# Both MLPs' matrix products by seven products of quarters in place of eight

## The chip, the cores and the metric

The kernel runs on one core of one Trainium2 chip. The metric is the device time of one launch in microseconds (us). Before the change it is 2720.57 us, the median of three runs (2720.34 to 2721.82).

The engines are named as in the profile: PE does matrix products (PEld loads their weights), DVE, ACT and POOL work on vectors, SP issues most of the DMA transfers. A queue with a q behind the name (SPq) is that engine's instruction queue.

## The reference, cut to what matters

Two transformer blocks run one after the other on 1024 tokens of width 1024. Each ends in an MLP of width 4096, with a residual; the attention and mixer parts ahead of the MLPs, the norms and the final norm are not touched by the change.

```
# block 1
h = rmsnorm(x, g_mlp)
hid = square(relu(h @ w_mlp_in))          # [1024,1024] @ [1024,4096]
x = x + hid @ w_mlp_out                   # [1024,4096] @ [4096,1024]
# block 2: mod = silu(c) @ w_ada + b_ada, cut in six (sh1, sc1, gt1, sh2, sc2, gt2)
x = x + gt1 * mixer(rmsnorm(x) * (1 + sc1) + sh1)
h = rmsnorm(x, g_ffn) * (1 + sc2) + sh2
x = x + gt2 * (square(relu(h @ w_ff1)) @ w_ff2)
return rmsnorm(x)
```

Everything is float32. A float32 product is made of three faster ones: each operand is cut into a rounded part `hi` and the rest `lo`, and hi·hi, hi·lo and lo·hi are summed.

## The kernel before, in words

All activations lie transposed, features on the 128 partitions and tokens along the rows; `xT[hf]` holds the residual of token half hf (512 tokens), as 8 tiles of 128x512, and `HT[hf]` the normed input h as `hi` and `lo`. `gemm_T` (L421 to L423) issues, for each 128 rows of the inner dimension, three PE instructions of 128x128 weights by 128x512 activations. `wunit` fetches a block of weights (`wload`, L132: one DMA on SP), ACT casts it into `wh` (L133), and DVE, in some places POOL, subtracts that from it for `wl` (L134).

One function, `mlp`, does both MLPs. It goes over the width 4096 in eight chunks of 512. In a chunk the first product makes four tiles of hidden values (`g1`): for each half the 24 PE instructions, then relu from PSUM on ACT (L1159), square on DVE (L1161), the `hi` cast on ACT (L1162) and `lo` on DVE (L1163). They stay in SBUF. Then the second product goes over the 8 output tiles, each from 4 weight tiles, for both halves; DVE adds the result from PSUM to the residual (`upd`, L1066, or L1068 with the gate of block 2). In the last chunk the sums of squares for the next norm are collected (`Stat.add`, with a POOL addition, L1011, and DVE instructions such as L1009), and in block 2 the output is turned back.

Ahead of each MLP stands the output projection (`out_proj`). Its second half leaves work that `mlp` starts in its first chunk through `begin`: the norm's factor is spread over the partitions (L1037), and `make_h` (L1076 and L1080, in block 2 L1083) makes h of token half 1 on DVE and ACT. Until then PE works on token half 0. In block 1 the MLP also carries `ada`, the product of silu(c) with `w_ada`: 48 loads of 512 KB on SP and as many DVE instructions (L1136), in small steps (`tick`).

Each engine has one queue in program order. The order in which instructions of different parts stand in it was fixed by the scheduler that builds the program, from the order of the code; on the chip an instruction at the head of a queue that waits holds up all behind it.

Of the kernel before, what the change touches and what calls it, by code (L numbers as in the profile page):

```python
# [60 lines left out]
def block_kernel(ctx, tc, x, mem, positions, g_mix, w_in, b_gate, sinks, g_mem, w_mem_kv, w_proj_swa, w_proj_dsa,  # L61
# [1055 lines left out]
    def ada(modp):  # L1117
# [10 lines left out]
        for g in range(6):  # L1128
            acc = modp([P, D], tag="ada", bufs=1)
            for k in range(DC):  # L1130
                w = modp([P, D], tag="adaw", bufs=2)
# [6 lines left out]
            m8 = mod[:, g * 8:(g + 1) * 8]  # L1138
            for j0 in (0, 4):
                pt = tp_bank()  # L1140
                for j in range(4):
                    T.transpose(pt[:, j * P:(j + 1) * P], acc[:, (j0 + j) * P:(j0 + j + 1) * P], ident)
                V.tensor_reduce(m8[:, j0:j0 + 4], pt.rearrange("p (j q) -> p j q", j=4), axis=AX.X, op=OP.add)
            V.tensor_tensor(m8, m8, bada[:, g * 8:(g + 1) * 8], op=OP.add)

    def mlp(pool, w1, w2, upd, post, begin, tick=lambda: None, gains=None, each=lambda i, e: None,
# [4 lines left out]
        NC_ = DFF // 512  # L1151

        def g1(units, f, hfs, hid, mid=None):
            accs = [(hf, mm_bank()) for hf in hfs]
            gemm_T(accs, units, h_rhs, mid=mid)
            for hf, a in accs:
                sl = halves(hf)
                r = pool([P, 512], tag="ml_r", bufs=2)
                A.activation(r, a, AF.Relu)  # L1159
                q = pool([P, 512], tag="ml_q", bufs=2)  # L1160
                V.tensor_tensor(q, r, r, op=OP.mult)  # L1161
                A.copy(hid[f][0][:, sl], q)  # L1162
                V.tensor_tensor(hid[f][1][:, sl], q, raw(hid[f][0][:, sl]), op=OP.subtract)  # L1163

        for c in range(NC_):
            hid = [(pool([P, S], F32R, tag="hid_hi", bufs=4), pool([P, S], F32R, tag="hid_lo", bufs=4))
                   for _ in range(4)]
            if c == 0:
                us = [[wunit(w1, 0, DC, f * P, P)] for f in range(3)]
                for hf in range(2):  # L1170
                    for f in range(3):
                        g1(us[f], f, [hf], hid, begin[1] if (hf, f) == (0, 1) else None)
                        if (hf, f) == (0, 0):
                            begin[0]()
                g1([wunit(w1, 0, DC, 3 * P, P)], 3, [0, 1], hid)
# [5 lines left out]
            def rhs(k, hf):  # L1181
                return hid[k][0][:, halves(hf)], hid[k][1][:, halves(hf)]
            if c < NC_ - 1:
                for e in range(DC):
                    u = [wunit(w2, c * 4, 4, e * P, P)]
                    accs = [(hf, mm_bank()) for hf in range(2)]
                    gemm_T(accs, u, rhs)
                    for hf, a in accs:
                        upd(e, hf, a)
                    if e % 2:  # L1190
                        tick()
            else:
                prev = None
                for i, (hf, t0, n) in enumerate(parts):
                    st = Stat(pools["stm"], gains, n)
                    sl = slice(t0, t0 + n)
                    for e2 in range(DC // 2):
                        hi, lo = wunit(w2, c * 4, 4, e2 * 256, 256, G)
                        for e in range(2):
                            a = mm_bank()[:, :n]  # L1200
                            gemm_T([(hf, a)], [(hi[:, :, e * P:(e + 1) * P], lo[:, :, e * P:(e + 1) * P])],
                                   lambda k, hf: tuple(z[:, sl] for z in rhs(k, hf)))
                            if e2 or e:
# [580 lines left out]
```

## Time and profile before

| what | value |
|---|---|
| median of three runs | 2720.57 us |
| the profiled execution, its own time | 2720.76 us |
| its span, first to last instruction | 2719.0 us |
| PE busy | 2650.9 us, 97% |
| DVE, ACT, POOL busy | 1439.7, 919.0, 339.1 us (53%, 34%, 12%) |
| MLP of block 1, first relu (L1159) to last residual addition (L1066) | starts 884.0 and 1596.0 us |
| MLP of block 2, first relu to last residual addition (L1068) | starts 2001.3 and 2709.9 us |
| DMA, mean over the span | 76 GB/s |

The profile counts an engine as busy while an instruction runs on it, waiting for a lock or a port included. The end of a matrix product is modelled, so one shows about 0.39 us although the next starts after 0.23; the time of a series is read from the starts. The granted clock of PE is a share of full speed, 1.00 being 2.4 GHz and 0.50 being 1.2 GHz.

### The profile page before, as it was taken

The page shows a single profiled execution, that of the slowest core. Times are in us where ns is not written, and L with a number is a line of the kernel's source. Part 1 is how long each engine was busy: PE and PEld are TensorE (multiplying, and loading weights), DVE is VectorE, ACT ScalarE, POOL GpSimd, SP SyncE. Part 2 cuts the span into 40 slices and gives each one's busy share as a digit, 9 for nine tenths or more (in the row PEclk, how much of TensorE's full clock was granted, in tenths as well). Part 3 has the DMA queues.
Part 4 walks back from the last instruction along what each step waited for, and adds up shares of the span by engine and source line. Part 5 has one row for each costly group of instructions (what it writes and reads, how often), then busy time and mean ns, then how long its engine had stood idle before and what let it go on. Part 6 is the DMA issues. An engine that isn't in the chain of part 4 may idle for free.

```text
span 2719.0 us, 34329 instructions
## 1 busy us (share of the span) xinstructions
PE 2650.9 (97%) x13328; PEld 2227.8 (82%) x13328; DVE 1439.7 (53%) x2836; ACT 919.0 (34%) x1826; POOL 339.1 (12%) x337
## 2 busy tenths in 40 slices
PE   7999999899999999999999989999999999999997
PEld 6899987788878888888888867888788888888886
DVE  7685878834455634553453476556553333333335
ACT  6575764335334221222212232332432122211223
POOL 3011123321001000000000331111310000000006
PEclk9999999999999999999999999999999999999999
DMA  3121022311154313331331124221421211121123
GB/s 114 53 61 40 26 80 88 93 57 41 63 165 124 109 45 114 117 102 49 109 101 55 55 59 148 63 78 39 139 70 54 59 36 47 51 58 47 39 62 124
DMA packets 263735, 206.41 MB, mean 76 GB/s; under 512 B 9468, under 2 KB 239636, under 8 KB 263572
## 3 DMA queue, kind: packets, MB, share of 16 engines
q1 hardware_dynamic: 255108, 180.25, 22.0%
q10 hardware_dynamic: 8464, 23.96, 2.6%
q8 instruction: 105, 1.72, 0.3%
q14 instruction: 58, 0.48, 0.1%
HBM read 185.24 MB, written 18.94 MB: 75 GB/s over the span
## 4 chain that ended last, share of the span: by engine, by line
PE 70%; DVE 4%; DMA 2%; ACT 1%; issue 1%; POOL 1%; POOLq 0%; SPq 0%; ACTq 0%; DVEq 0%
PE mm L422 19%; PE mm L423 19%; PE mm L421 19%; PE mm L1304 2%; PE mm L1306 2%; PE mm L1305 2%; PE tp L914 1%; DVE st_acc L1009 1%; PE mm L902 1%; DMA adaw<-in_w_ada_dram 1%; DVE h_lo L1083 0%; ACT wh L133 0%; DVE t L1076 0%; PE fl L273 0%; PE fl L271 0%
## 5 line engine op out<-in xcount | busy, mean ns | idle before, releaser
L423 PE MATMUL mm<-h_hi,wl 128*128 128x512 f32 x1248 | 486.0, 389 | 1.1 <-POOL wl L134 1.1
L133 ACT CAST wh<-wr 128x1024 fp32r<-128x1024 f32 (+3 forms) x303 | 254.8, 842 | 687.3 <-PE mm L422 579.5
L421 PE MATMUL mm<-h_hi,wh 128*128 128x512 f32 x1248 | 486.3, 390 | 0.6 <-ACT ft L280 0.6
L422 PE MATMUL mm<-h_lo,wh 128*128 128x512 f32 x1248 | 485.6, 389 | 0.0
L422 PE MATMUL mm<-hid_lo,wh 128*128 128x512 f32 (+1 forms) x1056 | 405.4, 384 | 3.7 <-DVE hid_lo L1163 3.7
L421 PE MATMUL mm<-hid_hi,wh 128*128 128x512 f32 (+1 forms) x1056 | 407.2, 386 | 0.0
L423 PE MATMUL mm<-hid_hi,wl 128*128 128x512 f32 (+1 forms) x1056 | 404.9, 383 | 0.0
L1161 DVE TENSOR_TENSOR ml_q<-ml_r 128x512 f32<-128x512 f32 x128 | 88.1, 688 | 419.5 <-ACT ml_r L1159 419.5
L134 POOL TENSOR_TENSOR wl<-wr,wh 128x1024 fp32r<-128x1024 f32 (+5 forms) x60 | 124.0, 2070 | 1465.7 <-ACT wh L133 1464.0
L423 PEld LDWEIGHTS mm<-h_hi,wl 128*128 128x128 f32 x1248 | 234.3, 188 | 51.3 <-POOL wl L134 2.0
L421 PEld LDWEIGHTS mm<-h_hi,wh 128*128 128x128 f32 x1248 | 234.3, 188 | 49.6 <-ACT ft L280 0.8
L422 PEld LDWEIGHTS mm<-h_lo,wh 128*128 128x128 f32 x1248 | 234.3, 188 | 48.4
L134 DVE TENSOR_TENSOR wl<-wr,wh 128x1024 fp32r<-128x1024 f32 (+2 forms) x243 | 235.5, 969 | 49.7 <-ACT wh L133 46.0
L422 PEld LDWEIGHTS mm<-hid_lo,wh 128*128 128x128 f32 x1056 | 198.8, 188 | 43.4 <-DVE hid_lo L1163 5.2
L423 PEld LDWEIGHTS mm<-hid_hi,wl 128*128 128x128 f32 x1056 | 198.8, 188 | 38.8
L421 PEld LDWEIGHTS mm<-hid_hi,wh 128*128 128x128 f32 x1056 | 198.8, 188 | 38.6
L1159 ACT ACTIVATE ml_r<-mm 128x512 f32<-128x512 f32 x128 | 76.8, 600 | 448.4 <-PE mm L423 448.4
L1068 DVE SCALAR_TENSOR_TENSOR x<-mm,mod,x 128x512 f32<-128x512 f32 (+1 forms) x152 | 105.7, 722 | 224.0 <-PE mm L423 224.0
L1304 PE MATMUL mm<-h_hi,wh 128*128 128x512 f32 x320 | 132.1, 413 | 0.5 <-DVE kn L1337 0.5
L1306 PE MATMUL mm<-h_hi,wl 128*128 128x512 f32 x320 | 126.7, 396 | 3.3 <-DVE wl L134 3.3
L1305 PE MATMUL mm<-h_lo,wh 128*128 128x512 f32 x320 | 126.0, 394 | 0.0
L1066 DVE TENSOR_TENSOR h_hi<-mm,h_hi 128x512 f32<-128x512 f32 x72 | 49.6, 689 | 124.5 <-PE mm L423 124.5
(474 smaller groups left out, 4573.8 us busy)
## 6 DMA issues: line engine op xcount, KB each, us to landing
adaw<-in_w_ada_dram SPq DMA_DIRECT2D x48, 512.0 KB
wr<-in_w_ff_dram SPq DMA_DIRECT2D x44, 512.0 KB
wr<-in_w_in_dram SPq DMA_DIRECT2D x42, 512.0 KB
wr<-in_w_out_dram SPq DMA_DIRECT2D x32, 512.0 KB
wr<-in_w_mlp_in_dram SPq DMA_DIRECT2D x32, 512.0 KB
wr<-in_w_mlp_out_dram SPq DMA_DIRECT2D x56, 256.0 KB
wr<-in_w_ff_dram SPq DMA_DIRECT2D x56, 256.0 KB
wr<-in_w_in_dram SPq DMA_DIRECT2D x20, 256.0 KB
```

What stands on the lines that cost most here:

```text
L133: A.copy(hi, r)
L134: (eng or V).tensor_tensor(lo, r, raw(hi), op=OP.subtract)
L421: mm(a, hi, r_hi, start=(i == 0), stop=False)
L422: mm(a, hi, r_lo, start=False, stop=False)
L423: mm(a, lo, r_hi, start=False, stop=(i == n - 1))
L1066: V.tensor_tensor(d, a, d, op=OP.add)
L1068: V.scalar_tensor_tensor(d, a, scale[:, e:e + 1], d, op0=OP.mult, op1=OP.add)
L1159: A.activation(r, a, AF.Relu)
L1161: V.tensor_tensor(q, r, r, op=OP.mult)
L1304: mm(a, hi[:, k, :], r_hi, start=(k == 0), stop=False)
L1305: mm(a, hi[:, k, :], r_lo, start=False, stop=False)
L1306: mm(a, lo[:, k, :], r_hi, start=False, stop=(k == DC - 1))
```

## The change

Both products of both MLPs are cut into quarters: inner dimension and output dimension in two, as 2x2 blocks, with the tokens as the other matrix's columns, again in two. One level of Strassen's scheme (in the form with reused sums) makes the four result blocks from seven products of blocks instead of eight. The price is sums and differences of the operands and of the results.

**First product.** The eight inputs are prepared once. `make_h` still makes h of token half 0 (B11, B21). For half 1 a new function `make_t` makes the four other operands as `hi` and `lo` tiles: T1, t2, t3, t4, of which t2 to t4 (`TQ`) go to a new pool. The loop then has 16 turns `m`, each for 128 rows of both output quarters. A turn loads three weight blocks of 512 KB: `e2` (as `wr`), `e1` (as `we`, one buffer) and, through `first_two` for a later turn, the block of `e1` a second time (as `wr`). POOL makes four weight sums of 128x512 (L1272 to L1275). Seven products follow, of 12 PE instructions each (84 in a turn; before, 96 for the same rows). Their sums are five DVE additions from PSUM (L1259, L1284, L1289, L1294, L1301), one DVE addition in SBUF, and a POOL addition (L1285); relu and square now stand on ACT. Four further POOL subtractions (L1305 three times, L1307) make the operands of the second product from the hidden values. The seven resulting tiles of 256 KB go to DRAM (`save`, L1247, on SP).

**Second product.** It goes over the width in four chunks. In each the seven operands are read back (1 MB each), cast on ACT and split, one half on DVE, the other on POOL (L1333); the four weight quarters (1 MB each) get eight 128x1024 sums on POOL; the seven products have 48 PE instructions each (336 in a chunk; before 384 for the same width). DVE adds results to the residual and to `U`, and POOL adds `U` to the residual (`upd_u`, L1352).

**Moved along.** The residual is saved to DRAM in `out_proj` and read back between the two products, since its tiles serve as scratch in the first. `ada` has steps of half the size and twice their number, six in each turn of the first product of block 1; whatever is left is done between the products. The spread of the norm's factor goes to another kind of PSUM bank.

What stands in a queue changes most on POOL. In the MLP of block 2 its queue held, between the factor of the norm ahead of it (L127) and the last chunk's weight splits (L134), nothing:

```order
L1011 TENSOR_TENSOR st_acc_3242_16963<-st_acc_3242_16963,t_3283_17222 128x512
L1011 TENSOR_TENSOR st_acc_3242_16963<-st_acc_3242_16963,t_3288_17258 128x512
L127 TENSOR_TENSOR st_r_17369<-st_r_17369,mhalf_73 128x4
L134 TENSOR_TENSOR wl_21505<-wr_21506,wh_21504 128x1024
L134 TENSOR_TENSOR wl_21550<-wr_21551,wh_21549 128x1024
```

Now there stand nine instructions for each turn of the first product. This is POOL in the middle of them; `x_3179` and `x_3180` are the tiles of the residual that serve as scratch:

```order
L1285 TENSOR_TENSOR x_3180_16953<-x_3179_16952,x_3180_16953 128x512
L1305 TENSOR_TENSOR x_3180_16953<-x_3179_16952,x_3180_16953 128x512
L1305 TENSOR_TENSOR x_3180_16953<-x_3180_16953,x_3179_16952 128x512
L1305 TENSOR_TENSOR x_3180_16953<-x_3180_16953 128x512
L1272 TENSOR_TENSOR sa_18151<-wr_18147 128x512
L1307 TENSOR_TENSOR x_3180_16953<-x_3180_16953 128x512
L1273 TENSOR_TENSOR sa_18151<-sa_18151,we_18149 128x512
L1274 TENSOR_TENSOR we_18149<-we_18149,wr_18147 128x512
L1275 TENSOR_TENSOR we_18149<-we_18149,sa_18151 128x512
L1285 TENSOR_TENSOR x_3180_16953<-x_3179_16952,x_3180_16953 128x512
```

The subtractions of turn m (L1305, L1307) stand ahead of the weight sums of turn m+2 (L1272 to L1275), and these ahead of the addition in turn m+1 (L1285).

SP's queue held only weight loads there, one behind the other; here are some of the first chunk and of the next:

```order
L132 DMA wr_17321<-in_w_ff_2_dram 128x8x128
L132 DMA wr_17327<-in_w_ff_2_dram 128x8x128
L132 DMA wr_17573<-in_w_ff_2_dram 128x8x128
L132 DMA wr_17641<-in_w_ff_2_dram 128x4x128
L132 DMA wr_17675<-in_w_ff_2_dram 128x4x128
```

Now the seven saves of a turn stand between its three loads (`ml_` are the tiles in DRAM):

```order
L1247 DMA ml_q_3183_16959<-x_3180_16953 128x512
L1247 DMA ml_t_3184_16960<-x_3180_16953 128x512
L1239 DMA wr_18293<-in_w_ff_2_dram 128x8x128
L1247 DMA ml_q_3188_16964<-x_3180_16953 128x512
L1247 DMA ml_q_3186_16962<-x_3180_16953 128x512
L1247 DMA ml_t_3187_16963<-x_3180_16953 128x512
L1247 DMA ml_t_3185_16961<-x_3180_16953 128x512
L1247 DMA ml_t_3189_16965<-x_3180_16953 128x512
L1239 DMA we_18295<-in_w_ff_2_dram 128x8x128
L1239 DMA wr_18320<-in_w_ff_2_dram 128x8x128
```

The load of `we` for turn m+2 stands behind the save of t4 of turn m (`ml_t_3189`).

In the opening of block 1's MLP DVE had `make_h` in a block of 16 instructions, which begins so:

```order
L1163 TENSOR_TENSOR hid_lo_9074<-ml_q_9126,hid_hi_9073 128x512
L1076 SCALAR_TENSOR_TENSOR t_1887_9161<-h_lo_8329,cols_75,sc_9156 128x512
L1076 SCALAR_TENSOR_TENSOR t_1888_9165<-h_lo_8329,cols_75,sc_9156 128x512
L1076 SCALAR_TENSOR_TENSOR t_1889_9169<-h_lo_8329,cols_75,sc_9156 128x512
L1080 TENSOR_TENSOR h_lo_9062<-t_1887_9161,h_hi_9061 128x512
```

Now it has `make_t`, 36 instructions, which ends so; `q_9100` and its like are parts of `TQ`, `sc_9268` is a product of `first_two`:

```order
L1120 TENSOR_TENSOR q_9104<-t_1898_9230,q_9103 128x512
L1130 TENSOR_TENSOR h_lo_8329<-h_lo_8329 128x512
L1120 TENSOR_TENSOR h_lo_9085<-h_lo_8329,h_hi_9084 128x512 x3
L1120 TENSOR_TENSOR q_9100<-t_1899_9240,q_9099 128x512
L1120 TENSOR_TENSOR q_9104<-t_1900_9242,q_9103 128x512
L1120 TENSOR_TENSOR h_lo_9085<-h_lo_8329,h_hi_9084 128x512
L1120 TENSOR_TENSOR q_9102<-h_lo_8329,q_9101 128x512 x4
L1259 TENSOR_TENSOR h_hi_8328<-sc_9268,h_hi_8328 128x512
```

The addition that empties `first_two`'s PSUM bank (L1259) stands behind all of it.

The diff, cut to its core; line numbers of the new code in the text are those of the changed kernel:

```diff
+    def make_t(pool, dst, src, rs, gain, shift=None):
...
+        for c in range(4):
+            z = first(c)
+            norm(c)
+            V.tensor_tensor(z, src(c), z, op=OP.subtract)
+            split_to(hi1[:, c, :], lo1[:, c, :], z)
+        for c in range(4):
+            norm(4 + c)
+            z, z4 = first(c), first(4 + c)
+            V.tensor_tensor(src(c), src(4 + c), src(c), op=OP.subtract)
+            G.tensor_tensor(z, src(c), z, op=OP.add)
+            split_to(TQ["t2"][0][:, c, :], TQ["t2"][1][:, c, :], z)
+            G.tensor_tensor(z4, z4, z, op=OP.subtract)
+            split_to(TQ["t4"][0][:, c, :], TQ["t4"][1][:, c, :], z4)
+        for c in range(4):
+            split_to(hi1[:, 4 + c, :], lo1[:, 4 + c, :], src(4 + c))
+        for c in range(4):
+            split_to(TQ["t3"][0][:, c, :], TQ["t3"][1][:, c, :], src(c))
...
-                for f in range(4):
-                    g1([wunit(w1, 0, DC, c * 512 + f * P, P)], f, [0, 1], hid)
-                    tick()
...
+        def first_two(m, mid=None):
+            s1, q11 = s1s[m % 4], q11s[m % 5]
+            u = parts_of(w_of(wp, 2 * m, "wr", 2))
...
+        for m in range(NM):
+            u2, q11, s5 = s1s[m % 4], q11s[m % 5], s5s[m % 2]
+            e2 = w_of(wp, 2 * m + 1, "wr", 2)
+            e1 = w_of(wep, 2 * m, "we", 1)
+            sa = wep([P, DC, P], tag="sa")
+            G.tensor_tensor(sa[:, 0:4], e2[:, 0:4], e2[:, 4:8], op=OP.add)
+            G.tensor_tensor(sa[:, 4:8], sa[:, 0:4], e1[:, 0:4], op=OP.subtract)
+            G.tensor_tensor(e1[:, 0:4], e1[:, 0:4], e2[:, 0:4], op=OP.subtract)
+            G.tensor_tensor(e1[:, 4:8], e1[:, 4:8], sa[:, 4:8], op=OP.subtract)
+            ua = parts_of(sa)
+            a = mm_bank()
+            product(a, half(ua, 0), T1)
+            A.copy(s5, a)
+            if m and m + 3 < NM:
+                first_two(m + 3)
+            a = mm_bank()
+            product(a, half(ua, 1), TQ["t2"])
+            V.tensor_tensor(u2, a, u2, op=OP.add)
+            G.tensor_tensor(o["q12"], u2, s5, op=OP.add)
+            ub = parts_of(e1)
...
+            V.tensor_tensor(o["q12"], a, o["q12"], op=OP.add)
+            relu2(o["q12"])
+            save("q12", m, o["q12"])
...
+            u4 = parts_of(e2[:, 4:8])
+            a = mm_bank()
+            product(a, u4, TQ["t4"])
+            V.tensor_tensor(u3, a, u3, op=OP.add)
+            relu2(u3)
+            save("q21", m, u3)
+            for n, p_, q_ in (("t1", q11, o["q12"]), ("t3", u3, q11), ("t2", u3, o["t1"])):
+                G.tensor_tensor(o[n], p_, q_, op=OP.subtract)
+                save(n, m, o[n])
+            G.tensor_tensor(s5, s5, o["t2"], op=OP.subtract)
+            save("t4", m, s5)
+            tick()
...
+        def second(n, ch):
...
+            for c in (0, 2):
+                A.copy(hi[:, c:c + 2], r[:, c:c + 2])
+                (G if c else V).tensor_tensor(lo[:, c:c + 2], r[:, c:c + 2], raw(hi[:, c:c + 2]), op=OP.subtract)
+            return hi, lo
...
+            for e, wt in blocks(a11):
+                a = mm_bank()
+                product(a, wt, b)
+                A.copy(U[e], a)
+                upd(1, e, a)
...
+                    for c in (0, 2):
+                        q_ = slice(c, c + 2)
+                        G.tensor_tensor(a21[:, q_], a11[:, q_], a21[:, q_], op=OP.subtract)
+                        G.tensor_tensor(a11[:, q_], s_[:, q_], a11[:, q_], op=OP.subtract)
```

## Rows read from the trace of the kernel before

**Rows 1.** The page: busy time by engine, and the chain that ended last.

```profile
PE 2650.9 (97%) x13328; PEld 2227.8 (82%) x13328; DVE 1439.7 (53%) x2836; ACT 919.0 (34%) x1826; POOL 339.1 (12%) x337
...
PE 70%; DVE 4%; DMA 2%; ACT 1%; issue 1%; POOL 1%; POOLq 0%; SPq 0%; ACTq 0%; DVEq 0%
```

**Rows 2.** Stretches: length, busy PE, PEld, DVE, ACT, POOL, granted clock, DMA share, GB/s.

```profile
1200.00:1300.00 100.00, 100.00 (x447) 82.90 (x446) 49.38 (x66) 18.91 (x30) 0.00 (x0) 1.00 0.36 109
2400.00:2500.00 100.00, 100.00 (x443) 82.80 (x442) 36.24 (x52) 18.92 (x30) 0.00 (x0) 1.00 0.17 48
```

**Rows 3.** Waits of PE from 860 to 1600: total us, times, longest.

```profile
PE tp L1026 <- DVE st_acc L1011: 3.8, 1, 3.8
PE mm L422 <- DVE hid_lo L1163: 1.9, 2, 1.7
```

**Rows 4.** Instructions of PE in order of time: start, length.

```profile
999.78 0.39 PE L423 MATMUL mm<-h_hi,wl 128*128 128x512 f32 x1
...
1007.94 0.39 PE L423 MATMUL mm<-h_hi,wl 128*128 128x512 f32 x1
```

**Rows 5.** Groups by line and shape, POOL: busy us, mean ns, idle before.

```profile
L134 POOL TENSOR_TENSOR wl<-wr,wh 128x1024 fp32r<-128x1024 f32 x39 | 96.8, 2484 | 1409.5 <-ACT wh L133 1407.8 <-PE mm L1584 1.5
...
L134 POOL TENSOR_TENSOR wl<-wr,wh 128x512 fp32r<-128x512 f32 x8 | 10.3, 1292 | 16.3 <-ACT wh L133 16.3
```

**Rows 6.** Groups by line and shape, DVE.

```profile
L134 DVE TENSOR_TENSOR wl<-wr,wh 128x1024 fp32r<-128x1024 f32 x123 | 155.6, 1265 | 44.7 <-ACT wh L133 40.9
...
L1068 DVE SCALAR_TENSOR_TENSOR x<-mm,mod,x 128x512 f32<-128x512 f32 x136 | 98.1, 750 | 216.6 <-PE mm L423 216.6
...
L134 DVE TENSOR_TENSOR wl<-wr,wh 128x512 fp32r<-128x512 f32 x112 | 76.6, 684 | 4.4 <-ACT wh L133 4.4
...
L1066 DVE TENSOR_TENSOR h_hi<-mm,h_hi 128x512 f32<-128x512 f32 x72 | 49.6, 689 | 124.5 <-PE mm L423 124.5
```

**Rows 7.** Groups by line and shape, ACT.

```profile
L133 ACT CAST wh<-wr 128x1024 fp32r<-128x1024 f32 x162 | 169.9, 1049 | 329.1 <-PE mm L422 242.3 <-issue 28.0 <-PE mm L1305 21.5
...
L1003 ACT ACTIVATE t<-x 128x512 f32<-128x512 f32 x21 | 13.3, 632 | 11.1 <-DVE x L1068 11.0
```

**Rows 8.** Instructions of DVE in order of time, end of block 1's MLP.

```profile
1547.65 2.45 DVE L1009 SCALAR_TENSOR_TENSOR st_acc<-t,gsq,st_acc 128x512 f32<-128x512 f32 x1 [0.74 <-ACT t L1003]
1550.03 0.68 DVE L1066 TENSOR_TENSOR h_hi<-mm,h_hi 128x512 f32<-128x512 f32 x1
1551.41 0.75 DVE L1009 SCALAR_TENSOR_TENSOR st_acc<-t,gsq,st_acc 128x512 f32<-128x512 f32 x1 [0.70 <-ACT t L1003]
```

**Rows 9.** Instructions of POOL in the same stretch.

```profile
1547.17 2.39 POOL L134 TENSOR_TENSOR wl<-wr,wh 128x1024 fp32r<-128x1024 f32 x1 [5.07 <-ACT wh L133]
1549.52 1.74 POOL L1011 TENSOR_TENSOR st_acc<-st_acc,t 128x512 f32<-128x512 f32 x1
```

**Rows 10.** SP's queue: two issues of 512 KB, the first at 2068.87.

```profile
2068.87 6.54 SPq L132 DMA_DIRECT2D wr<-in_w_ff_dram  x2
```

**Rows 11.** Stretches behind the first of these issues.

```profile
2072.00:2072.50 0.50, 0.50 (x3) 0.39 (x3) 0.25 (x1) 0.00 (x0) 0.00 (x0) 1.00 0.39 115
2072.50:2073.00 0.50, 0.50 (x4) 0.42 (x3) 0.50 (x2) 0.30 (x1) 0.00 (x0) 1.00 0.00 0
```

**Rows 12.** DVE in order of time, block 1's opening: first and last rows of `make_h`.

```profile
888.31 2.07 DVE L1076 SCALAR_TENSOR_TENSOR t<-h_lo,cols,sc 128x512 f32<-128x512 f32 x3 [1.22 <-PE sc L1037]
...
897.83 1.29 DVE L1080 TENSOR_TENSOR h_lo<-t,h_hi 128x512 fp32r<-128x512 f32 x2
```

**Rows 13.** Stretches of the kernel's beginning.

```profile
20.00:22.00 2.00, 0.45 (x4) 0.21 (x2) 2.00 (x4) 1.70 (x3) 0.54 (x1) 0.62 0.49 78
22.00:24.00 2.00, 1.74 (x6) 1.74 (x7) 2.00 (x5) 1.42 (x5) 0.00 (x0) 0.50 0.94 367
24.00:26.00 2.00, 2.00 (x9) 2.00 (x9) 2.00 (x8) 1.98 (x3) 0.00 (x0) 0.50 1.02 368
```

**Rows 14.** The longest wait of PE in the execution.

```profile
PE tp L478 <- DMA rows<-in_g_mem_dram: 6.2, 1, 6.2
```

More of the change, by code (lines that the diff above doesn't have):

```diff
@@ L1033, in spread @@
     def spread(r):
-        b = sc_bank()
+        b = tp_bank()
         for j in range(4):
@@ L1083, in make_h, with mlp_dram, with_x_out, both @@
                 V.scalar_tensor_tensor(lo, n, shift(c), raw(hi), op0=OP.add, op1=OP.subtract)
+    NM = DFF // (2 * P)
+    OUTS = ("q12", "t1", "t2", "q21", "t3", "q22", "t4")
+    TQ = {}
+    def mlp_dram(pool):
+        d = {n: pool([P, NM, 512], tag=f"ml_{n}") for n in OUTS}
+        d["x"] = pool([P, DC, S], tag="ml_x")
+        return d
+    def with_x_out(d, upd):
+        def both(e, hf, a):
+            r = upd(e, hf, a)
+            nc.sync.dma_start(d["x"][:, e, halves(hf)], r)
+            return r
+        return both
+    def make_t(pool, dst, src, rs, gain, shift=None):
+        (hi0, lo0), (hi1, lo1) = HT[0], dst
+        def norm(c):
+            V.scalar_tensor_tensor(src(c), src(c), gain(c), rs, op0=OP.mult, op1=OP.mult)
+            if shift is not None:
+                A.activation(src(c), src(c), AF.Identity, bias=shift(c))
+        def first(c):
+            z = pool.t512()
+            G.tensor_tensor(z, raw(hi0[:, c, :]), raw(lo0[:, c, :]), op=OP.add)
+            return z
+        def split_to(hi, lo, r):
+            A.copy(hi, r)
+            V.tensor_tensor(lo, r, raw(hi), op=OP.subtract)
+        for c in range(4):
[15 more added lines that the diff above has]
+            split_to(TQ["t3"][0][:, c, :], TQ["t3"][1][:, c, :], src(c))
     xT = [hB([P, DC, 512], tag=n) for n in ("h_hi", "h_lo")]
-    stp = Pool("stp", side="right")
+    stp = Pool("stp", side="right", n512=4)
     xtp = Pool("xtp", side="right")
@@ L1137, in ada @@
                 yield
[L1138 to L1146, printed above, removed]
-            parts=((0, 0, 512), (1, 0, 512))):
[L1151 to L1175, printed above, removed]
-            else:
-                for f in range(4):
-                    g1([wunit(w1, 0, DC, c * 512 + f * P, P)], f, [0, 1], hid)
-                    tick()
[L1181 to L1203, printed above, removed]
-                                each(i, 2 * e2 + e - 1)
-                            elif prev:
-                                each(i - 1, DC - 1)
-                            st.add(upd(2 * e2 + e, hf, a, sl))
-                            if prev and 2 * e2 + e in (0, 2):
-                                next(prev)
-                    prev = post(i, st)
-                each(len(parts) - 1, DC - 1)
-                for _ in prev:
-                    pass
@@ L1260, in begin1, with middle1, tick1 @@
         stp.close()
+        ada_["it"] = ada(pools["mod"])
+    def middle1():
+        for _ in ada_["it"]:
+            pass
         pools["stm"] = Pool("stm", side="right", n512=2)
-        pools["mod"] = Pool("modp", side="right")
-        ada_["it"] = ada(pools["mod"])
-    mlp(hidp, w_mlp_in[0], w_mlp_out[0], add_to(xT), post_mlp1, (lambda: next(pend), begin1),
-        lambda: next(ada_["it"], None), gsq)
-    hidp.close()
+    def tick1():
+        for _ in range(6):
+            next(ada_["it"], None)
+    pools["mod"] = Pool("modp")
+    mlp(hBp, xT, mlp_d, w_mlp_in[0], w_mlp_out[0], None, post_mlp1, (lambda: next(pend), begin1), middle1, tick1, gsq)
     pools["mod"].close()
+    drm.close()
     HT[:] = h2
```

234 lines of the change are left out of this document (211 added, 23 removed).

## The prediction

> **What bounds the kernel now.** I read the page's busy times and its chain of waits first: PE is busy for 2650.9 us, 97% of the span, and 70% of the chain that ended last runs over PE, against 4% over DVE and 1% over POOL [rows 1]. Then the stretches inside the two MLPs: PE is busy in all of 100 us at a granted clock of 1.00, while DVE is busy for 36 to 49 us, ACT for 19, POOL not at all, and DMA has a share of 0.17 to 0.36 [rows 2]. Then PE's waits: in the whole of block 1's MLP they come to 3.8 and 1.9 us [rows 3]. So the MLPs stand at PE's own pace, and a PE instruction that goes is worth its pitch, as long as nothing else becomes the bound. The pitch is read from starts, since the shown lengths overlap: from 999.78 to 1007.94 lie 36 steps, so 0.2267 us each [rows 4].
>
> **The change part by part.** Each of the four products has 8 x 32 x 2 x 3 = 1536 PE instructions, 348.2 us. The change leaves seven eighths, 1344 or 304.7 us, so 4 x 43.5 = 174.1 us of PE go. That is a gain only where the rest keeps up with 84 x 0.2267 = 19.04 us for a turn of the first product and 336 x 0.2267 = 76.2 us for a chunk of the second. What is added stands on POOL and DVE, which until now had room.
>
> Prices: POOL takes 1.29 us for a 128x512 addition and 2.48 for 128x1024, somewhat lengthened by waits (2.39 alone) [rows 5, 9]; DVE 0.68 for 128x512 and 1.27 for 128x1024 with both inputs in SBUF, 0.69 to 0.75 from PSUM [rows 6]; ACT 1.05 for a weight cast and 0.63 for one activation [rows 7].
>
> Both engines must share something. A DVE instruction with two SBUF inputs that takes 0.75 us alone took 2.45 when POOL was in a 2.39 us subtraction, and ended about 0.54 us behind it; POOL's next addition, begun while that one still ran, took 1.74 in place of 1.29; the DVE addition from PSUM beside it kept its 0.68 [rows 8, 9]. So I add POOL's time and DVE's two-SBUF time, and leave PSUM additions out. The Trainium skill says the same in "SBUF — State Buffer", section "Who interferes with whom": two SBUF inputs contend with a POOL instruction that reads SBUF and one of them waits in full, an instruction with one SBUF input does not. By that the PSUM additions are free of it, and the trace agrees (0.68 us); if they were not, a chunk of the second product would have some 23 us more of shared time and each MLP would lose about 90 us more.
>
> First product, shared time of a turn: POOL 9 x 1.29 = 11.6; DVE three weight splits of 1.27, one of 0.68, the sum of s5 0.68, together 5.2. That is 16.8 us in block 2, under PE's 19.04. In block 1 six steps of `ada` at 0.75 come on top: 21.3, over it.
>
> But the sequence decides more than the sum. From the queues follows a loop in which no product of PE stands, once per turn: POOL's t3, t2, the weight sum of turn m+2 and t4 (4 x 1.29 = 5.2); then SP saves t4 and only then issues the load of `we` for turn m+2. A 512 KB load issued at 2068.87 still moved data behind 2072.0 and none behind 2072.5 [rows 10, 11]: 3.5 us. Then POOL's three weight sums that need it and, behind them in its queue, the addition of q12 of turn m+1 (5.2). Then DVE's addition (0.69), relu and square on ACT (1.26), the cast of a weight block that stands next on ACT (1.05), its split on DVE (1.27, behind POOL's t1 at the shared port, up to 1.29), DVE's last sum (0.69), relu and square of q21 (1.26), which t3 of turn m+1 needs: 7.5. A split of 1.27 falls among POOL's sums. Together 5.2 + 3.5 + 5.2 + 7.5 + 1.3 = 22.7 us a turn in block 2, against 19.04. In block 1 two `ada` loads stand ahead of `we` on SP and about three `ada` steps inside the loop on DVE: some 2 + 2.3 more, 27. A turn without `first_two` lacks a cast and a split: 20.4 and 24.5. Bounds: without any wait at the port 20.1, with an estimated 0.2 for the hand-over at each of a dozen steps 25 in block 2; in block 1 21.3 (the shared time alone) to 30.
>
> A first product is four `first_two` (96 instructions, 21.8 us), twelve full turns and four short ones. Block 2: 21.8 + 272.4 + 81.6 = 375.8, which is 27.6 more than now. Block 1: 21.8 + 324 + 98 = 443.8, 95.6 more.
>
> Opening: `make_h` for half 1 took DVE from 888.31 to about 899.1, hidden behind PE [rows 12]. `make_t` has 28 two-SBUF DVE instructions (19.2), 8 norms (6.0) and 20 POOL additions, of which 16 fall behind the norm's factor (20.6). At the shared port that makes 39.8 us. PE has 48 products' instructions left after the spread (10.9 us) before it needs t3, and DVE empties `first_two`'s banks only behind all of `make_t`. So PE stands for about 29 us, bounds 14 (DVE alone sets it) and 37. The 3.8 us that it waits there now goes with it: I take +25 per block, 50.
>
> Second product, a chunk: POOL seven splits and eight sums of 2.39 and twelve additions of 1.29, 51.3; DVE's two-SBUF splits 7 + 14 of 1.22 to 1.27, 25.6; shared 76.9, as much as PE's 76.2. Two in-order engines that hold each other up do not reach 100% of a shared port: I take 82 us, bounds 76.2 and 92. Against 87.05 now that is -5.05 a chunk, -40 in all. ACT (some 35 us) and DMA stay far off. DMA: seven saves and three loads are 3.4 MB a turn, 5 MB in block 1; at a share of 1.02 the queues moved 368 GB/s [rows 13], by which that is 9 to 14 us of a turn's 19, so I cost the traffic only where a wait names it. The first weights of the second product go to buffers that t2 to t4 hold until the first ends: +3 per block, 6; below nothing is excluded.
>
> Sum against the profiled execution: 27.6 + 95.6 + 50 - 40 + 6 = +139; 2720.76 + 139 = 2860 us. Its own time is 0.2 us from the median, so the forecast for the median is 2860. With all bounds at one end it would be 2650 or 3037; half-way in each term gives 2760 to 2945, the likeliest case's own range.
>
> **Rivals.**
> *The load is there in time.* If `we` has landed when POOL comes to it, the loop loses 3.5 us: 19.2 in block 2, PE's pace, and 21.3 in block 1. Then the first products are at -28 and +5, with opening, transition and second product as above: -7, and with the second product at PE's pace -54. Time 2700, range 2665 to 2730. For it: DMA is idle for most of the time now. Against: the load is issued behind a save that waits for POOL, one buffer only.
>
> *PE stays the bound (the other side).* If POOL's and DVE's work is overlapped so well that a turn is under 19.04 us and a chunk at 76.2, the 174.1 us are gained less opening and transition: 2720.8 - 174 + 56 = 2603, range 2560 to 2640. The mechanism is that PE can run ahead over its three and two PSUM banks and over the weights of two turns, so that the loop above is cut; it decides where a turn without port and transfer waits, 16.6 us by the same terms, is what happens. For it: DVE is idle for half of each stretch and POOL for all of it [rows 2]. Against: the shared time is over 19.04 in block 1 and at 100% in the second product.
>
> *The clock falls in the new gaps.* After a wait of 6.2 us at the start, PE ran at 0.50 for some 6 us [rows 13, 14]: three microseconds lost behind one such wait. Waits in each of the 32 turns that are as long would cost up to 96 us on top: 2956, range 2900 to 3050. Against: a turn's gap of 4 to 8 us is cut into several waits, and PE has slack in the loop. The Trainium skill ("TensorE: Matmul & The Clock Gate", section "HAM oscillation — how this bites in real kernels") warns that a kernel with a gap in each step pays the change of clock in each; here the trace shows it for a single wait only.
>
> **How the numbers follow.** Likeliest case 0.60, load in time 0.18, PE the bound 0.12, clock 0.08, something else 0.02. The range 2600 to 2950 leaves out about half of the PE case and of the clock case and the upper edge of the likeliest, 0.17 in all. Faster by over 0.2% (5.4 us, about what a measurement of this kernel tells from none): the PE case, two thirds of the load case and the rest of chance, 0.26; within it 0.03; slower 0.71.
>
> **What would show it.** The profile after should have POOL busy for 60 to 80% of the first products' stretches, PE for 70 to 85%, with waits of PE for DVE weight splits and PSUM additions, of POOL for the DMA of `we`, and DVE's 0.68 us instructions lengthened to over 1. At the opening PE should stand for some 29 us for `make_t`. The turns should be 22.7 and 27 us apart, the chunks 82. A turn of 19 us with PE at 100% makes the loop wrong; a chunk over 87 makes the second product's gain wrong; a granted clock under 1.00 in the turns speaks for the third rival. The forecast falls if turns come at PE's pace in both blocks.

## The result and the profile after

The changed kernel takes 2892.1 us (median of four runs, 2885.7 to 2897.1) against 2720.45 us for the kernel before, run beside it (median of four): a ratio of 1.063, 95% interval 1.0607 to 1.0654. It is slower by 171.6 us. Forecast were 2860 us and a range of 2600 to 2950.

The page of the changed kernel, busy time by engine and then the chain that ended last:

```profile
PE 2577.5 (89%) x12560; PEld 2133.1 (74%) x12560; DVE 1827.8 (63%) x3006; ACT 1214.8 (42%) x2146; POOL 1266.2 (44%) x853
...
PE 39%; POOL 11%; DVE 10%; DMA 9%; issue 7%; ACT 3%; SPq 1%; POOLq 0%; DVEq 0%; ACTq 0%
```

Against [rows 1] PE's busy time fell by only 73 of the 174 us that its missing 768 instructions are worth. Most of the rest is the clock: by the trace, 182 us of its busy time passed at a granted clock of 0.50, against 15 before, and at half speed that is 84 us more for the same work. PE's share of the chain went from 70% to 39%; POOL, DVE, DMA and issue took it over. Three stretches, columns as in [rows 2] (block 2's first product, its second, block 1's first):

```profile
2184.00:2284.00 100.00, 90.11 (x369) 71.65 (x369) 38.42 (x43) 40.16 (x59) 52.49 (x39) 0.95 0.48 154
2600.00:2700.00 100.00, 93.15 (x389) 76.17 (x390) 68.07 (x63) 39.93 (x45) 71.71 (x33) 0.95 0.39 137
1100.00:1200.00 100.00, 83.90 (x348) 67.52 (x348) 58.36 (x70) 38.36 (x56) 52.62 (x36) 0.91 0.64 200
```

No engine is full in any of them, so no engine's busy time alone names the bound; the next thing to look for is a loop of waits. Here it is in block 2. POOL in order of time, from t4 of one turn (L1307) to that of the next:

```profile
2230.64 1.29 POOL L1307 TENSOR_TENSOR x<-x 128x512 f32<-128x512 f32 x1
2236.88 1.29 POOL L1273 TENSOR_TENSOR sa<-sa,we 128x512 f32<-128x512 f32 x1 [4.95 <-DMA we<-in_w_ff_dram]
2238.26 1.29 POOL L1274 TENSOR_TENSOR we<-we,wr 128x512 f32<-128x512 f32 x1
2239.50 2.27 POOL L1275 TENSOR_TENSOR we<-we,sa 128x512 f32<-128x512 f32 x1
2241.73 1.29 POOL L1285 TENSOR_TENSOR x<-x,x 128x512 f32<-128x512 f32 x1
2245.16 1.27 POOL L1305 TENSOR_TENSOR x<-x,x 128x512 f32<-128x512 f32 x1 [2.13 <-ACT x L1244]
2249.53 1.29 POOL L1305 TENSOR_TENSOR x<-x,x 128x512 f32<-128x512 f32 x1 [3.09 <-ACT x L1244]
2250.77 1.30 POOL L1305 TENSOR_TENSOR x<-x 128x512 f32<-128x512 f32 x1
2252.21 1.28 POOL L1272 TENSOR_TENSOR sa<-wr 128x512 f32<-128x512 f32 x1
2253.45 1.29 POOL L1307 TENSOR_TENSOR x<-x 128x512 f32<-128x512 f32 x1
```

SP's queue beside it: the save of t4, then the load:

```profile
2231.96 0.32 SPq L1247 DMA_DIRECT2D ml_t<-x  x1
2232.37 0.39 SPq L1239 DMA_DIRECT2D we<-in_w_ff_dram  x1
```

DVE beside it, the part that follows POOL's L1285:

```profile
2239.30 1.33 DVE L1219 TENSOR_TENSOR wl<-sa,wh 128x1024 fp32r<-128x1024 f32 x1 [4.25 <-ACT wh L1218]
...
2243.06 0.69 DVE L1289 TENSOR_TENSOR x<-sc,x 128x512 f32<-128x512 f32 x1 [2.43 <-POOL x L1285]
...
2246.05 1.47 DVE L1219 TENSOR_TENSOR wl<-wr,wh 128x1024 fp32r<-128x1024 f32 x1 [0.97 <-ACT wh L1218]
2247.43 0.68 DVE L1301 TENSOR_TENSOR x<-mm,x 128x512 f32<-128x512 f32 x1
```

Read from the top: t4 ends at 2231.9, the save goes at 2231.96 and the load of `we` at 2232.37; POOL stands until 2236.88; its sums and L1285 end at 2243.02 (L1275 took 2.27 in place of 1.29 beside a DVE split); DVE's L1289 follows, then ACT and DVE up to L1301, and the second L1305 (t3) starts at 2249.53. The two L1307 lie 22.8 us apart. Over twelve turns, from the first L1301 of block 2 to the thirteenth, a turn takes 23.2 us:

```profile
2178.77 0.68 DVE L1301 TENSOR_TENSOR x<-mm,x 128x512 f32<-128x512 f32 x1
...
2457.56 0.68 DVE L1301 TENSOR_TENSOR x<-mm,x 128x512 f32<-128x512 f32 x1
```

In block 1 it takes 25.6 us, read in the same way.

### The profile page after: what moved, and what is told of

It reads as the page before. It is cut to its first block, busy times and chain, and to the rows that moved or that the text cites. A ratio compares the mean times of both kernels' runs of the same rounds, so it can differ in the third digit from the quotient of the medians.

```text
span 2892.7 us, 34868 instructions
## 1 busy us (share of the span) xinstructions
PE 2577.5 (89%) x12560; PEld 2133.1 (74%) x12560; DVE 1827.8 (63%) x3006; ACT 1214.8 (42%) x2146; POOL 1266.2 (44%) x853
## 4 chain that ended last, share of the span: by engine, by line
PE 39%; POOL 11%; DVE 10%; DMA 9%; issue 7%; ACT 3%; SPq 1%; POOLq 0%; DVEq 0%; ACTq 0%
PE mm L1226 4%; PE mm L1225 4%; PE mm L1224 4%; PE sc L1224 3%; PE mm L423 3%; PE mm L422 3%; PE mm L421 3%; PE sc L1225 2%; PE sc L1226 2%; PE mm L1559 2%; DVE wl L1219 2%; PE mm L1561 2%; PE mm L1560 2%; POOL we L1275 2%; DMA adaw<-in_w_ada_dram 2%
## 5 line engine op out<-in xcount | busy, mean ns | idle before, releaser
L1224 PE MATMUL mm<-h_hi,wh 128*128 128x512 f32 (+1 forms) x624 | 256.5, 411 | 50.9 <-ACT wh L1218 49.8
L1224 PE MATMUL sc<-h_hi,wh 128*128 128x512 f32 x512 | 214.8, 420 | 62.5 <-ACT wh L1218 25.6
L1226 PE MATMUL mm<-h_hi,wl 128*128 128x512 f32 (+1 forms) x624 | 254.3, 408 | 16.1 <-DVE wl L1219 16.0
L1219 DVE TENSOR_TENSOR wl<-q,wh 128x1024 fp32r<-128x1024 f32 x116 | 211.6, 1825 | 61.1 <-ACT wh L1218 59.5
L1226 PE MATMUL sc<-h_hi,wl 128*128 128x512 f32 x512 | 210.2, 411 | 6.7 <-DVE wl L1219 6.6
L1224 PEld LDWEIGHTS mm<-h_hi,wh 128*128 128x128 f32 x624 | 125.0, 200 | 82.1 <-ACT wh L1218 57.3
L1225 PE MATMUL mm<-h_lo,wh 128*128 128x512 f32 x416 | 172.2, 414 | 0.0
L1224 PE MATMUL mm<-q,wh 128*128 128x512 f32 x384 | 150.9, 393 | 22.2 <-ACT q L1119 22.2
L1225 PE MATMUL mm<-q,wh 128*128 128x512 f32 x384 | 151.6, 395 | 19.0 <-DVE q L1120 19.0
L1226 PEld LDWEIGHTS mm<-h_hi,wl 128*128 128x128 f32 x624 | 124.6, 200 | 53.0 <-DVE wl L1219 27.7
L1225 PE MATMUL sc<-h_lo,wh 128*128 128x512 f32 (+1 forms) x400 | 159.1, 398 | 0.0
L1226 PE MATMUL mm<-q,wl 128*128 128x512 f32 x384 | 150.5, 392 | 2.7 <-DVE wl L1219 2.7
L134 POOL TENSOR_TENSOR wl<-wr,wh 128x1024 fp32r<-128x1024 f32 (+5 forms) x40 | 78.1, 1958 | 162.6 <-ACT wh L133 159.2
L1333 POOL TENSOR_TENSOR h_hi<-h_lo,h_hi 128x1024 fp32r<-128x1024 f32 x38 | 110.6, 2911 | 78.8 <-ACT h_hi L1332 78.0
L1225 PE MATMUL mm<-h_hi,wh 128*128 128x512 f32 (+1 forms) x368 | 142.3, 387 | 2.3 <-DVE h_hi L1333 2.3
L1559 PE MATMUL mm<-h_hi,wh 128*128 128x512 f32 x320 | 132.0, 412 | 0.8 <-DVE kn L1592 0.8
```

Of the source, the lines that this page charges most:

```text
L1219: (eng or V).tensor_tensor(lo, r, raw(hi), op=OP.subtract)
L1224: mm(a, wt[0][:, k], b[0][:, k, sl], start=(k == 0), stop=False)
L1225: mm(a, wt[0][:, k], b[1][:, k, sl], start=False, stop=False)
L1226: mm(a, wt[1][:, k], b[0][:, k, sl], start=False, stop=(k == 3))
L1333: (G if c else V).tensor_tensor(lo[:, c:c + 2], r[:, c:c + 2], raw(hi[:, c:c + 2]), op=OP.subtract)
L1559: mm(a, hi[:, k, :], r_hi, start=(k == 0), stop=False)
```

## The experiments

Times are for the whole kernel. A turn is the mean of the first twelve distances between starts of L1301 of one block, a chunk the distance between the first L1414 of one chunk and that of the next (or of the same statements where an edit moves the line numbers).

**The load of `we` on another queue.**

```diff
-            nc.sync.dma_start(r, w1[...])
+            (nc.scalar if tag == "we" else nc.sync).dma_start(r, w1[...])
```

> Only the load of we goes to ACT's DMA queue in place of SP's, so that it no longer stands behind the save of t4. Theory (the loop over POOL, the save, the load and POOL again sets a turn): POOL's wait for the DMA of we, now 55.8 us over eleven turns of block 2, nearly goes, and a turn of block 2 falls from 22.97 to 19 to 20 us, at PE's pace; block 1 from 25.6 to 22 to 24, since ada is untouched; the whole by 60 to 100 us, to 2790 to 2830. Rival (PE with its lowered clock, or the shared port, sets the turn): the wait for we goes but turns stay within 1 us of 22.97 and the time within 25 us of 2892.

Measured: 2825.7 us, a turn of 20.0 in block 2 and 23.7 in block 1, inside the forecast ranges. POOL's wait for that load in eleven turns, in the changed kernel and then in this one:

```profile
POOL sa L1273 <- DMA we<-in_w_ff_dram: 55.8, 11, 5.4
```

```profile
POOL sa L1273 <- DMA we<-in_w_ff_dram: 20.2, 11, 3.4
```

35.6 us over eleven turns is 3.2 a turn, and the turn fell by 3.2. No vector work was moved. The loop sets the turn in block 2; the rival falls. POOL still waits 1.8 us a turn for the load.

**The five sums on DVE.**

```diff
-            G.tensor_tensor(o["q12"], u2, s5, op=OP.add)
+            V.tensor_tensor(o["q12"], u2, s5, op=OP.add)
...
-                G.tensor_tensor(o[n], p_, q_, op=OP.subtract)
+                V.tensor_tensor(o[n], p_, q_, op=OP.subtract)
...
-            G.tensor_tensor(s5, s5, o["t2"], op=OP.subtract)
+            V.tensor_tensor(s5, s5, o["t2"], op=OP.subtract)
```

> The addition of q12 and the four subtractions t1 to t4 of each turn of the first product are done by DVE in place of POOL; POOL keeps the four weight sums. Theory (the loop sets the turn): the loop is cut where POOL's weight sums stood between t4 and q12, so turns fall to 19 to 20 us in block 2 and 21 to 24 in block 1, the whole to 2780 to 2830. Rival (the shared port's total sets it): the port's sum falls only from 16.8 to 13.8 us a turn, under PE's 19.04 in both, so it would predict no change in block 2. Rival (DVE becomes the bound): DVE's own time goes to about 14 us a turn, and waits of PE for DVE's PSUM additions grow; turns of 21 to 23.

Measured: 2780.1 us; turns of 19.4 in block 2 and 22.2 in block 1. A stretch of block 2's first product:

```profile
2150.00:2250.00 100.00, 100.00 (x443) 82.81 (x442) 66.50 (x77) 49.14 (x72) 32.63 (x21) 1.00 0.57 183
```

PE is full again and its clock back at 1.00, although DVE works 28 us more in 100 than before the edit. With the run above, which left the vector work alone, this rules out the port's total, DVE and the clock as the cause in block 2; cutting the loop is enough. 112 us come back by an edit that adds nothing and takes nothing away, 87 of them in the twelve turns of each block. In block 1 the turn stays 3 us above PE's pace.

**The second product's splits and additions on DVE.**

```diff
-                (G if c else V).tensor_tensor(lo[:, c:c + 2], ...)
+                V.tensor_tensor(lo[:, c:c + 2], ...)
...
-                (V if last and hf == 0 else G).tensor_tensor(t_, t_, u, op=OP.add)
+                V.tensor_tensor(t_, t_, u, op=OP.add)
```

> Second product alone: the lo split of the operands read back and the additions of U to the residual are all done by DVE; POOL keeps the eight weight sums of a chunk. Theory (the port shared by POOL and two-SBUF DVE instructions sets the chunk): shared time falls from 76.9 to about 61, DVE's weight splits come back from 2.0 to 3.3 towards 1.3 to 1.8 us, and the chunk falls from 83.6 to 76.5 to 79 us, the whole by 40 to 60 us. Rival (DVE's own queue is what PE waits for): DVE's own time rises from about 49 to 66 us of a chunk, waits of PE for L1339 and L1341 stay or grow, chunk 83 to 88.

Measured: 2849.6 us, 42.5 less, but chunks of 81.3 in block 1 (85 to 83.5 before the edit) and 82.1 to 83.7 in block 2 (83.1 to 84.2). DVE's weight splits in three chunks of block 2, first in the changed kernel, then here:

```profile
L1219 DVE TENSOR_TENSOR wl<-q,wh 128x1024 fp32r<-128x1024 f32 x42 | 70.5, 1678 | 26.3 <-ACT wh L1218 25.4
```

```profile
L1219 DVE TENSOR_TENSOR wl<-q,wh 128x1024 fp32r<-128x1024 f32 x42 | 56.7, 1351 | 10.7 <-ACT wh L1218 9.8
```

The port did lengthen them, by 0.3 us on average, but the chunks came out between theory (76.5 to 79) and rival (83 to 88). The whole gain lies in the forecast range, but in block 2 14.6 of its 23 us came at the passage from the first product to the second; in block 1 most came in the chunks. What stays in a chunk of block 2 is a wait of PE for DVE's L1341 of 3.8 to 5 us, which the rival had named.

**`make_t` on DVE**: the three `G.tensor_tensor` of the diff above become `V.tensor_tensor`.

> The twenty POOL additions of make_t are done by DVE (0.69 us each in place of 1.29). Theory (POOL and DVE share the port there, so that their times add up): DVE alone then needs 39 us, as much as both together now (39.8), and PE's stand at each opening stays at 24 to 32 us; the whole within 10 us of 2892. Rival (the two engines ran side by side and the chain between them set the length): with all on one engine the opening grows by 10 us or more per block.

Measured: 2879.0 us, 13 less, a little outside the 10 that were forecast. The first L1301 of a block comes 3.5 and 7.3 us earlier, and PE's waits at the openings come to 25.4 and 21.8 us in place of 28 (in block 2 mostly because the wait for the norm's factor fell from 5.4 to 0.5). Nothing grew by 10, so the rival falls: DVE alone does in no more time what both did together. That their times added up at the port shows in the changed kernel, where DVE's splits for t2 and t4 in block 2's opening took twice their 0.68 us:

```profile
L1120 DVE TENSOR_TENSOR q<-t,q 128x512 fp32r<-128x512 f32 x8 | 10.8, 1371 | 2.4 <-ACT q L1119 1.9
```

**`ada`'s transposes a turn later** (with the sums on DVE).

```diff
+                if k == 5 and g:
+                    turned(g - 1, prev)
```

where `turned` holds the transposes, the reduction and the sum that stood at the end of the group.

> As the run with the five sums on DVE, and the four PE transposes that close a group of ada come one turn later, from a second accumulator. Theory (PE, with its queue in order, waits for ada's last DVE step of a group, 44.9 us in all in the changed kernel): the turns of block 1 that took 22 to 24 us fall to 19 to 20 like the others, its first product from 395 to 350 to 365 us, the whole from 2780 to 2740 to 2755. Rival (the shared port, over 19.04 us a turn in block 1, sets these turns): they stay at 22 to 24 and the time within 10 us of 2780.

Measured: 2776.4 us, turns of 22.9 in block 1: the theory missed, the rival's times held. PE's waits from 930 to 1290 before this edit, then with it (the lines of this kernel are higher by 6):

```profile
PE tp L1199 <- DVE ada L1194: 21.5, 6, 6.3
PE mm L1224 <- ACT wh L1218: 10.7, 4, 7.1
...
PE mm L1226 <- DVE wl L1219: 5.0, 6, 1.3
```

```profile
PE mm L1232 <- DVE wl L1225: 25.0, 19, 3.3
PE mm L1230 <- ACT wh L1224: 13.6, 9, 9.6
```

The wait for `ada` went and the same time came back as a wait for weight splits. The transposes stood where PE would have waited anyway. Whether the port makes the splits late, as the rival has it, this run does not show.

**More banks for the second product of a chunk** (on top of the splits on DVE).

```diff
-                a = sc_bank()
+                a = tp_bank() if ch else sc_bank()
```

> As the run with the second product's splits and additions on DVE, and the second of its seven products, whose results DVE adds twice, goes to the three banks that hold transposes elsewhere, in place of two, in all chunks but each block's first. Theory (what is left in the chunk is PE waiting 3.8 to 5 us for DVE to empty one of two banks, and PE's clock behind that wait): chunks fall from 82 to 77 to 79 us, the whole from 2850 to 2820 to 2835. Rival (DVE's queue as a whole is late there, so that more banks only move the wait): chunks stay at 81 to 83.

Measured: 2851.6 us, chunks of 79.8 to 83.8: no gain in the whole, the rival held. PE's wait stood at the sixth product, not the second.

**All edits together, without and with the openings and banks.** The first also moves the read-back of the residual behind the first three weight quarters.

> All that helped so far together, without the banks: the five sums, the second product's splits and additions on DVE, ada's transposes a turn later, and the residual read back behind the first weight quarters of the second product in place of before them. Theory: the gains of the single runs add: 2892 - 112 (sums) - 43 (second product) - 30 (ada) - 10 to 20 (transition) is 2690 to 2715, which is below the kernel before. Rival (DVE, which now carries it all, becomes the bound): first products at 20 to 22 a turn, over 2730.

> As the run before, with make_t's additions on DVE and the extra banks as well. Theory: some 10 us less for the openings and 15 for the chunks, so 2665 to 2695, faster than the kernel before by 1 to 2%. Rival (DVE is the bound): no gain over the run before.

Measured: 2742.6 and 2729.7 us (the second at a ratio of 1.0031, interval 1.002 to 1.0042, still a little slower than the kernel before). Both miss their forecasts by some 30 us. The gain of 30 set down for `ada` did not exist. DVE is busy for 67 of 82 us in a chunk and 78 of 100 in block 1's turns; that it no longer follows everywhere is likely, but not shown. By blocks, from the first to the last PE instruction, 743.2 and 696.1 us against 826.8 and 775.0 in the changed kernel.

**Two ways to free SP's queue in block 1.** The load of `we`, or `ada`'s loads, on ACT's queue; both with the chunk's sixth product on the three other banks.

> As the run with all edits, but the load of we on ACT's queue, and of the second product's chunk the sixth product (operand q22), not the second, has the three other banks. Theory (in block 1 the turns of 22 to 24 us are now set by SP's queue, in which the weight loads stand behind ada's loads that wait for DVE: POOL waited 70.7 us for we and 59.0 for wr): turns of block 1 fall from 22.6 to 20 to 21.5 us; and the chunk's wait of 3 to 4 us sits at the sixth product, so chunks fall from 82 to 78 to 80. Together 2690 to 2710, faster than the kernel before. Rival (DVE and the port set the turns of block 1): turns stay over 22 and the time over 2715.

> As the run before, but ada's loads on ACT's queue in place of the load of we. Theory (SP's queue): SP is free of waits for DVE, so turns of block 1 fall to 19.5 to 21 us, 2685 to 2710, if ACT, which now waits for ada's buffers in its own queue, is not late. Rival (ACT becomes late): its casts come later, PE waits for ACT's wh, and turns are 22 or more.

Measured: 2730.2 and 2732.6 us, turns of 22.9 and 23.0 in block 1, chunks of 82.1 in block 2. Both rivals held. With the sums on DVE, moving these loads to another queue gained nothing, and three banks in place of two helped the chunk neither at the second product nor at the sixth.

**`ada` with one load per group.**

> As the run with all edits (2729.7), but ada loads one of its eight 256 KB blocks per group and uses it for all eight steps, so that the modulation is not the reference's; its DVE steps are all there. It tells apart what holds block 1's turns at 22.6 us where block 2's take 19.4. Theory A (DVE and the port: six steps of ada a turn are 4.5 us more of DVE's two-SBUF time): turns stay at 22 to 23, the whole within 10 us of 2730. Theory B (the loads of ada: 1.5 MB more a turn on the DMA and SP's waits for their buffers): turns fall to 19.4 to 20.5, the whole to 2690 to 2705.

Measured: 2713.6 us, turns of 21.8 in block 1. That is between both theories: seven eighths of the loads gone give 0.8 us of the 3.2 by which these turns exceed block 2's. A stretch of block 1:

```profile
1100.00:1200.00 100.00, 93.18 (x399) 74.13 (x398) 84.91 (x103) 41.17 (x61) 30.81 (x20) 0.98 0.53 175
```

DVE is busy for 85 us of 100, the fullest of the vector engines. That `ada`'s DVE steps hold the rest is likely, but no run took them out, so what sets block 1's turns stays open.

**Seven products in block 2 alone**, with the edits that helped; block 1's MLP as before.

> The MLP of block 1 as in the kernel before (with ada in whole steps), that of block 2 by seven products with the edits that helped: sums, splits and residual additions and make_t on DVE, the read-back behind the first weight quarters, the sixth product of a chunk in the three other banks. Block 2's MLP took 714 us before and 693 in the run with ada's loads on ACT's queue, so the theory (the two MLPs are independent of each other) gives 2720.4 - 21 = 2700, range 2692 to 2708, faster by 0.4 to 1.0%. Rival (block 1 pays for something that is moved, such as the other PSUM bank of the norm's spread): 2710 or more.

Measured: 2699.6 us, ratio 0.9919, interval 0.9905 to 0.9933: faster than the kernel before by 20.4 us, as forecast. The page's first part:

```profile
PE 2588.7 (96%) x12944; PEld 2169.4 (80%) x12944; DVE 1686.6 (62%) x3072; ACT 1079.7 (40%) x2006; POOL 501.5 (19%) x421
```

384 PE instructions fewer than before are worth 87 us; 20 of them arrive. Of the others, PE's waits are 21.3 at the opening and 12.6 at the passage, and four chunks of 82.1 in place of 76.2 are another 24.

## Why the prediction was right, point by point

The mechanism of the turns was right and carried the forecast. That the whole came within 32 us of it is partly luck, since other terms were off by more and with both signs.

**The loop, right in mechanism and size in block 2.** The prediction put a turn at 22.7 us in block 2 and 27 in block 1; measured are 23.2 and 25.6. In the turn shown above, save and load take 4.95 in place of 3.5, POOL's sums 6.1 in place of 6.5 (the split among them counted), the chain on DVE and ACT 6.5 in place of 7.5, the subtractions 5.2 as forecast. The 0.2 us for a hand-over in the upper bound stood on no row; here SP issued the save 0.03 us after t4 had ended, and DVE began 0.04 after L1285. Two single edits, each at one place of the loop, bring block 2 to 20.0 and 19.4. In block 1 they leave 23.7 and 22.2, so there this loop is only a part of the turn. The first rival (load in time) was forecast to give 19.2 in block 2 and 21.3 in block 1; with the load issued earlier, though not yet in time, they were 20.0 and 23.7.

Of the signs that were named, POOL's wait for `we` came, and PE's for weight splits. POOL was busy for 52% in the turns, not 60 to 80, and PE for 90% in block 2, not 70 to 85; its share holds the slow stretches too.

**Openings, right in total.** 29 us were forecast per block. PE's waits there (block 2):

```profile
PE mm L1224 <- ACT q L1119: 13.1, 2, 11.2
PE mm L1225 <- DVE q L1120: 7.6, 2, 6.9
PE tp L1037 <- POOL st_r L127: 5.4, 1, 5.4
PE sc L1224 <- DVE x L1259: 1.6, 1, 1.6
```

Together 27.7 us, in block 1 28.3. For `make_t` itself it is 22.3 (all rows but the third), less than its 29; the third wait, 5.4, was not in the sum: the norm's factor stands on POOL behind four weight sums of the first turn, where before [rows 3] PE waited 3.8 us for another step of the norm. So the size came out right by two errors that cancel, which is luck.

**First products together.** From the first PE instruction to the last L1301 they take 401.6 us in block 2 (375.8 and 29 forecast) and 441.6 in block 1 (443.8 and 29). Block 1 is 31 us under: its turns are 1.4 us and its short turns some 4 us cheaper than taken, probably because `ada`'s steps partly fall where DVE has nothing else to do; no run tested that. Block 2's 3 us are two errors as well: its twelve turns took 6 more than forecast, its short ones 9 less.

**The passage between the products, mis-sized.** It was put at 3 us a block. PE's waits there in block 2:

```profile
PE sc L1224 <- ACT wh L1218: 13.4, 1, 13.4
PE sc L1224 <- DVE x L1341: 5.7, 1, 5.7
PE mm L1224 <- ACT wh L1218: 5.6, 1, 5.6
PE sc L1226 <- DVE wl L1219: 1.9, 2, 1.1
```

26.6 us, in block 1 36.3 (8.7 of it for `ada`). The weights for the second product's second step need buffers that the last turn holds, and then a load, two POOL sums, a cast and a split pass one after the other before PE has them; the prediction named the buffers and priced only a part of what follows. The place in SP's queue counts as well. In the changed kernel the third load of weights for the second product (L1363) stood behind the last turn's saves and the read-back of the residual, and POOL waited for it:

```profile
2515.75 2.94 SPq L1247 DMA_DIRECT2D ml_t<-x  x3
2518.78 2.88 SPq L1318 DMA_DIRECT2D x<-ml_x  x6
2521.71 0.43 SPq L1363 DMA_DIRECT2D q<-in_w_ff_dram  x1
```

```profile
2529.16 4.64 POOL L1388 TENSOR_TENSOR q<-q,q 128x1024 f32<-128x1024 f32 x2 [10.81 <-DMA q<-in_w_ff_dram]
```

With the second product's work on DVE, the program had this load ahead of those saves, 2.5 us before block 2's last L1301 in place of 12 behind it, and the wait of 13.4 fell to 1.8:

```profile
2480.26 0.49 SPq L1363 DMA_DIRECT2D q<-in_w_ff_dram  x1
```

So the buffers alone do not set it. With 57 us more than forecast this is the largest error. With chunks of 83.9 in place of 82 (+15) and the first products (-31 and -3) the errors come to +38; the forecast was low by 32. The 6 us between were not followed up.

**The second product, right in kind.** 82 us a chunk, 83.9 measured. Here POOL and DVE do hold each other up: DVE in the changed kernel,

```profile
2583.95 3.41 DVE L1333 TENSOR_TENSOR h_hi<-h_lo,h_hi 128x1024 fp32r<-128x1024 f32 x1
2587.28 1.28 DVE L1428 TENSOR_TENSOR u<-mm,u 128x512 f32<-128x512 f32 x2
2589.76 3.30 DVE L1219 TENSOR_TENSOR wl<-q,wh 128x1024 fp32r<-128x1024 f32 x1 [1.20 <-ACT wh L1218]
```

and POOL beside it:

```profile
2582.89 6.73 POOL L1405 TENSOR_TENSOR q<-q,q 128x1024 f32<-128x1024 f32 x2
2589.58 2.39 POOL L1333 TENSOR_TENSOR h_hi<-h_lo,h_hi 128x1024 fp32r<-128x1024 f32 x1
```

Splits of 1.2 us take 3.3 to 3.4, POOL's two sums 6.73 in place of 4.8, and the additions from PSUM between them keep their 0.68 each (two, overlapping by a little, in 1.28). The wait that costs PE time, 4.8 us a chunk, is for DVE's additions that stand behind such splits. That DVE's queue stays late there once the port is free was not in the prediction.

**The clock rival, a part only.** A wait in a turn of block 2, and the stretches around it:

```profile
2223.22 0.50 PE L1224 MATMUL mm<-h_hi,wh 128*128 128x512 f32 x1 [2.28 <-ACT wh L1218]
```

```profile
2222.00:2224.00 2.00, 0.73 (x2) 0.30 (x2) 1.03 (x2) 1.97 (x4) 1.28 (x1) 1.00 0.34 131
2224.00:2226.00 2.00, 1.28 (x5) 1.04 (x6) 1.94 (x3) 1.97 (x4) 0.00 (x0) 0.91 0.39 146
2226.00:2228.00 2.00, 2.00 (x7) 1.52 (x6) 0.56 (x1) 1.07 (x2) 1.32 (x2) 0.50 0.70 174
2228.00:2230.00 2.00, 2.00 (x8) 1.64 (x7) 0.00 (x0) 0.59 (x1) 1.79 (x2) 0.73 1.08 396
```

PE waited 2.3 us, then 0.8 more, and shortly after ran at 1.2 GHz for some 3 us. The Trainium skill ("TensorE: Matmul & The Clock Gate", section "HAM oscillation — how this bites in real kernels") describes a kernel in which the wait of each step makes the next step start at the slow clock. The trace agrees in part: the clock fell to 0.50, as in row three, in five of block 2's twelve turns. In those twelve turns 25.6 us of PE's busy time passed at 0.50, which costs 12.8 us or 1.1 a turn, against the 4.2 by which a turn exceeds PE's pace; and with the loop cut the clock was back at 1.00 without any step against it. In block 2's chunks it is 15 us in three, 2.5 us lost in each; with a wait of 4.8 that is the distance of 83.5 from 76.2. The rows that the prediction took for this rival [rows 13, 14] it misread. In the kernel before, the wait of 6.2 us ended at 6.15, and PE's clock was still at 1.00 from 16 to 20, after a stretch of shorter waits, before it fell:

```profile
16.00:20.00 4.00, 2.08 (x12) 1.44 (x11) 3.86 (x9) 3.39 (x6) 1.26 (x2) 1.00 0.07 14
```

The mean granted clock of the whole fell from 0.996 to 0.947.

## What to carry to other kernels

Fewer matrix instructions help only if what replaces them fits beside PE as a sequence, not just as a sum: write down, for one turn, the loop of waits over the in-order queues that contains no matrix product, with each DMA in it, and compare its length with PE's time for the turn. A load with one buffer that stands in a queue behind a save of the same turn can close such a loop; moving the load to another queue, or the cheap operations around it to another engine, can cut it. A second buffer was not tried. Where a stage has its own operands to prepare, price the whole chain at the passage (place in the queue, buffer, load, sum, cast, split), and look at each user of the stage apart: here the scheme, with the edits, pays in the block without `ada`; in the other it does not, and why is not settled.
